# A decoder layer with a product-key expert FFN: loads of the expert stage pinned in program order, own slots for the U tiles, gates read in parts

## The chip, the cores and the metric

The kernel runs on one core of one Trainium2 chip. What counts is the device time of one execution in microseconds (us). Of the kernel before, three runs are known: median 1809.51 us, from 1806.57 to 1817.64 us.

## The reference, cut to what matters

512 tokens of 1024 numbers pass through one layer: a mixer, and behind it an expert FFN in which every token picks, for each of 8 heads, 16 of 16,384 experts. Each expert has a row in `expert_u` and one in `expert_v`.

```python
q = (xc @ w_q).reshape(PEER_CHUNK, PEER_HEADS, 2, PEER_HALF)
s1 = einsum('thd,hnd->thn', q[:, :, 0], sub_keys_1)      # 128 keys per half
s2 = einsum('thd,hnd->thn', q[:, :, 1], sub_keys_2)
...                                                      # top 16 of both, top 16 of their sums
g = jax.nn.softmax(top_s, axis=-1)
u_sel = jnp.take(expert_u, idx, axis=0)
act = jax.nn.gelu(jnp.einsum('thkd,td->thk', u_sel, xc))
v_sel = jnp.take(expert_v, idx, axis=0)
return jnp.einsum('thk,thkd->td', g * act, v_sel)
...
h = h + hybrid_mixer(n, ...)
h = h + peer(rms_norm(h, norm_ffn), ...)
return rms_norm(h, norm_final)
```

All values are float32.

## The kernel before

**Arithmetic.** A float32 matrix product is done as three matmul passes over a high and a low part of each operand. A weight tile of 128x1024 float32 (512 KB) is loaded by SP's DMA queue into a slot `raw` (L80, four slots), ACT copies it to `whi` (L74), and VectorE (DVE) subtracts to get `wlo` (L75; for some tiles GpSimd, POOL, does that). `whi` and `wlo` have three slots each. TensorE (PE) then uses both.

**Expert FFN.** For the first 384 tokens (three groups of 128) the experts are not gathered: all 128 tiles of 128 experts are multiplied with all these tokens, and the result is weighted by a gate that is zero where an expert was not chosen. For tile j, `act_tile(j)` loads the U tile and makes the gelu of its products (24 matmuls, L89, L377), and `out_tile(j)` loads the V tile, multiplies the activations with the gates (DVE, L638), splits the product into `w_hi` (ACT, L74) and `w_lo` (DVE, L75), and adds 18 matmuls onto six PSUM banks `acc` (L645). The last 128 tokens are done by gathers: 128 indirect DMAs by POOL (L402), each bringing one row of U and V per token (1 MB, slot `row`, four of them), and on DVE a dot product with each (`junk`, L409) and a weighted sum (`yg`, L396), in a fixed order.

**Stages.** Mixer (0 to 500 us); queries and top 16 (500 to 690); decoding of the indices (690 to 765); the gates stage, which builds the gate matrix in 48 blocks of 8 tokens (L571 to L596: four DVE instructions, L564 and L566, and 16 small matmuls, L583 and L584, a block; every fourth block a DMA stores 2 MB, `stg`, into the DRAM array `gscr`, L592); the expert stage (1006 to 1798), and the closing normalisation `finish` (L612).

**Tiles done ahead.** The U tiles of 74 of the 128 j, the list `LAG`, are computed before the expert stage by `lag_tiles` (L382): 20 in the top-16 stage, 12 while decoding, 42 between the blocks of the gates stage. Of the first 12 (`keep`) the activations stay in SBUF; the others are stored to DRAM (`ascr`, L389) and read again in the expert stage into a slot `back` (L661, four slots), two tiles ahead in the program (`PRE = 2`).

**Order.** In the expert stage the program goes through j: read the `back` of j+2, compute the U tile of j if it was not done ahead, then `out_tile(j-1)`, then some gathered rows. The gates of four tiles are read by one DMA of 768 KB in runs of 512 bytes (`gt`, L634), two slots, at the `out_tile` that uses them first. PE runs in program order. A scheduler orders the other engines and SP's queue, except for instructions pinned by `keep_in_program_order`; each engine, and SP's queue, then works strictly in its order. A DMA whose slot is still in use blocks all behind it in SP's queue. SP's slot waits are mostly for the `wlo` that read a `raw` slot last.

Of the kernel before, what the change touches and what calls it, by code (L numbers as in the profile page):

```python
# [21 lines left out]
P = 128  # L22
D = 1024
# [13 lines left out]
NG = ND // TG  # L37
JG = 4
NL = 74
LAG = [j for j in range(P) if j * NL // P != (j - 1) * NL // P]  # L40
# [6 lines left out]
AR = 20  # L47
AD = 4
UP = 24
PRE = 2  # L50
C_VEC = dict(nm=0, nf=8, ca=16, rw=40, rb=80, brg=90, big=100, lam=110)
# [4 lines left out]
def layer(ctx: ExitStack, tc: tile.TileContext, a):  # L56
# [20 lines left out]

    def weights(src, k, eng=None):
        raw = ring.tile([P, k * P], F32, tag="raw", name="raw", bufs=4)
        SP.dma_start(raw, src)  # L80
        hi, lo = split(raw, [P, k * P], ("whi", "wlo"), ring, 3, eng)
        return hi.rearrange("p (k m) -> p k m", k=k), lo.rearrange("p (k m) -> p k m", k=k)
# [285 lines left out]

    def act_tile(j):
        u = weights(a["ut"][j], KD, G if j in LAG[:AR] else V)  # L370
        pa = bank("01", (P, S))
        mm3(pa[:, :ND], u, n2d)
        if j in LAG[:JK]:
            g = gp.tile([P, ND], F32, tag="keep", name="keep", bufs=JK)
        else:
            g = gp.tile([P, ND], F32, tag="gel", name="gel", bufs=3)
        A.activation(g, pa[:, :ND], AF.Gelu_apprx_tanh)  # L377
        return g
# [20 lines left out]
    def gathered(i, pin=False):  # L399

        r = gp.tile([P, 2 * D], F32, tag="row", name="row", bufs=4)
        ins = G.indirect_dma_start(  # L402
            out=r, out_offset=None, in_=a["uv"], in_offset=bass.IndirectOffsetOnAxis(ap=uidx[:, i : i + 1], axis=0)
        )
        if pin:
            tc.keep_in_program_order(ins)
        junk = gp.tile([P, D], BF16, tag="junk", name="junk", bufs=1)
        tc.keep_in_program_order(
            V.scalar_tensor_tensor(junk, r[:, :D], 1.0, n2tok, op0=ALU.mult, op1=ALU.mult, accum_out=dots[:, i : i + 1])  # L409
        )  # L410
# [140 lines left out]
    with tc.tile_pool(name="gates", bufs=1) as rp:  # L551
# [17 lines left out]
        blocks = [(t, t0) for t in range(NT) for t0 in range(0, P, TE)]  # L569
        ahead = rows_of(*blocks[0])  # L570
        for n, (t, t0) in enumerate(blocks):  # L571
            e2, eh, el = ahead
# [18 lines left out]
            if s0 + TE == TG:  # L591
                SP.dma_start(gscr[t * (P // TG) + c], stg)  # L592
            left = NL - AR - AD * NT
            lag_tiles((n + 1) * left // len(blocks) - n * left // len(blocks))
            for i in range(n * UP // len(blocks), (n + 1) * UP // len(blocks)):
                gathered(i)  # L596


# [4 lines left out]
    def residual(k):  # L603
        hk = ep.tile([P, S], F32, tag="hk", name="hk", bufs=2)
        SP.dma_start(hk, hscr[:, k, :])
        c = (k % 4) * P
# [4 lines left out]

    def finish(t, parts):  # L612
        sq = ep.tile([P, S], F32, tag="fsq", name="fsq", bufs=2)
        ss = ep.tile([P, 2], F32, tag="fss", name="fss", bufs=2)
        A.activation(sq, parts[0], AF.Square, accum_out=ss[:, 0:1])
        A.activation(sq, parts[1], AF.Square, accum_out=ss[:, 1:2])
        s1 = ep.tile([P, 1], F32, tag="fs1", name="fs1", bufs=2)
# [3 lines left out]
        o = ep.tile([P, D], F32, tag="fo", name="fo", bufs=2)  # L621
        for f in range(2):
            fs = slice(f * S, (f + 1) * S)
            V.scalar_tensor_tensor(o[:, fs], parts[f], s1, gfin[:, fs], op0=ALU.mult, op1=ALU.mult)
            SP.dma_start(a["out"][t * P : (t + 1) * P, fs], o[:, fs])
# [39 lines left out]
    work.append(lambda: finish(3, [yg[:, :S], yg[:, S:]]))  # L665
    share = [1.0 if j in LAG else RN for j in range(P)]
# [4 lines left out]
    for j in range(P + 1):  # L671
        if j < P:
            read_back(j + PRE)
            g = kept[j] if j in LAG else act_tile(j)
            part += share[j]
# [5 lines left out]
        while done < min(len(work), math.ceil(part * len(work) / total)):  # L681
            work[done]()
            done += 1
    for t in range(NT):
        finish(t, acc[t])

# [48 lines left out]
```

## Time and profile before

| | |
|---|---|
| median of 3 runs | 1809.51 us (1806.57 to 1817.64) |
| the profiled execution, its own time | 1809.08 us |
| its span in the trace | 1807.4 us |
| busy share PE, DVE, ACT, POOL | 96%, 71%, 42%, 18% |
| expert stage | 1006 to 1798 us |

The profile is one execution seen by the hardware profiler. The page gives the busy time of each engine; a table by windows gives it by stage, with the granted TensorE clock (PEclk, 1.00 is full) and the busy share of the 16 DMA engines. The list of waits groups an engine's idle time by what ended it: "DVE back L638 <- DMA back<-ascr" is DVE standing at the gate multiply until the read of `back` had landed. The chain of waits goes back from the last instruction to what released it, and shows which of these waits set the end; in it a DMA piece runs from its issue to its landing. 1.7 us of the execution lie outside the span.

### The profile page before, as it was taken

How to read it: one execution, taken by the hardware profiler on the slowest of the kernel's cores; microseconds unless marked ns; L12 is line 12 of the kernel's file. 1: busy time of each engine (PE TensorE's matmuls, PEld its weight loads, DVE VectorE, ACT ScalarE, POOL GpSimd, SP SyncE). 2: the span in 40 equal slices, each digit the busy share in tenths (PEclk: the TensorE clock that was granted, in tenths of full speed). 3: DMA queues.
4: the chain of work that ended last, by engine and by line, in shares of the span. 5: the costliest groups of instructions: out<-in, count | busy, mean ns of one | idle time of the engine just before them, and what ended most of it. 6: DMA issues, size and time to landing. Idle time of an engine off the chain costs nothing.

```text
span 1807.4 us, 24072 instructions
## 1 busy us (share of the span) xinstructions
PE 1736.7 (96%) x8861; PEld 1515.1 (84%) x8861; DVE 1286.5 (71%) x2345; ACT 763.8 (42%) x1290; POOL 320.2 (18%) x253
## 2 busy tenths in 40 slices
PE   8999999999989998999999899999899999999998
PEld 6888888888879887999999688788787878888786
DVE  7979442225578668899997777787676866787673
ACT  5774332222343335555554343344343433444353
POOL 0000000000145552023222111122121111122100
PEclk9999999999999998999999999999999999999999
DMA  4323223333433335579999988898898988898872
GB/s 164 114 82 111 96 79 95 107 105 94 134 114 96 103 120 199 171 307 357 376 367 369 347 309 312 297 332 313 283 322 295 323 289 309 310 344 313 308 239 72
DMA packets 147846, 410.06 MB, mean 227 GB/s; under 512 B 11536, under 2 KB 78864, under 8 KB 129680
## 3 DMA queue, kind: packets, MB, share of 16 engines
q1 hardware_dynamic: 129296, 274.30, 45.5%
q0 software_dynamic: 18432, 134.23, 19.2%
q8 instruction: 69, 1.13, 0.2%
q14 instruction: 49, 0.40, 0.1%
HBM read 366.93 MB, written 41.55 MB: 226 GB/s over the span
## 4 chain that ended last, share of the span: by engine, by line
PE 78%; DMA 9%; DVE 8%; issue 2%; ACT 2%; SPq 0%; DVEq 0%; ACTq 0%
PE ps L89 55%; PE acc L645 19%; DMA back<-ascr 5%; DMA gt<-gscr 3%; DVE wlo L75 3%; PE ps L583 1%; PE ps L584 1%; PE ps L517 1%; ACT whi L74 1%; PE ps L236 1%; DVE gel L638 1%; DMA gscr<-stg 1%; ACT w_hi L74 1%; DVE junk L409 1%; DVE nk L141 0%
## 5 line engine op out<-in xcount | busy, mean ns | idle before, releaser
L74 ACT ACTIVATE whi<-raw 128x1024 fp32r<-128x1024 f32 (+1 forms) x364 | 380.6, 1046 | 693.9 <-PE ps L89 479.5
L75 DVE TENSOR_TENSOR wlo<-raw,whi 128x1024 fp32r<-128x1024 f32 (+1 forms) x328 | 393.0, 1201 | 219.1 <-ACT whi L74 218.5
L89 PE MATMUL ps<-q_hi,whi 128*128 128x384 f32 (+1 forms) x1232 | 436.4, 354 | 11.6 <-ACT whi L74 8.9
L89 PE MATMUL ps<-q_hi,wlo 128*128 128x384 f32 (+1 forms) x1232 | 430.0, 349 | 6.1 <-DVE wlo L75 6.1
L89 PE MATMUL ps<-q_lo,whi 128*128 128x384 f32 (+1 forms) x1232 | 429.8, 349 | 0.3 <-DVE q_lo L143 0.3
L402 POOL DMA_INDIRECT row<-uv,uidx x128 | 210.2, 1642 | 766.9 <-DVE yg L396 757.5
L645 PE MATMUL acc<-whi,w_hi 128*128 128x512 f32 x768 | 245.9, 401 | 37.9 <-ACT w_hi L74 37.3
L89 PEld LDWEIGHTS ps<-q_hi,whi 128*128 128x128 f32 x1232 | 234.6, 190 | 24.3 <-ACT whi L74 10.2
L89 PEld LDWEIGHTS ps<-q_hi,wlo 128*128 128x128 f32 x1232 | 234.2, 190 | 17.1 <-DVE wlo L75 8.1
L89 PEld LDWEIGHTS ps<-q_lo,whi 128*128 128x128 f32 x1232 | 234.8, 191 | 11.1 <-DVE q_lo L143 0.7
L645 PE MATMUL acc<-wlo,w_hi 128*128 128x512 f32 x768 | 241.6, 396 | 0.0
L645 PE MATMUL acc<-whi,w_lo 128*128 128x512 f32 x768 | 240.9, 395 | 0.0
L645 PEld LDWEIGHTS acc<-whi,w_hi 128*128 128x128 f32 x768 | 144.9, 192 | 70.8 <-ACT w_hi L74 45.6
L645 PEld LDWEIGHTS acc<-wlo,w_hi 128*128 128x128 f32 x768 | 147.6, 192 | 32.2
L645 PEld LDWEIGHTS acc<-whi,w_lo 128*128 128x128 f32 x768 | 146.5, 191 | 31.5
L89 PE MATMUL ps<-n_hi,whi 128*128 128x512 f32 x432 | 168.4, 390 | 0.0
L89 PE MATMUL ps<-n_hi,wlo 128*128 128x512 f32 x432 | 168.2, 390 | 0.0
L89 PE MATMUL ps<-n_lo,whi 128*128 128x512 f32 x432 | 168.1, 389 | 0.0
L396 DVE SCALAR_TENSOR_TENSOR yg<-row,dots,yg 128x1024 f32<-128x1024 f32 x128 | 163.9, 1280 | 0.0
L409 DVE SCALAR_TENSOR_TENSOR junk<-row,n2tok 128x1024 bf16<-128x1024 f32 x128 | 156.0, 1219 | 0.0
L75 POOL TENSOR_TENSOR wlo<-raw,whi 128x1024 fp32r<-128x1024 f32 x36 | 87.2, 2424 | 349.8 <-ACT whi L74 349.8
L89 PEld LDWEIGHTS ps<-n_hi,wlo 128*128 128x128 f32 x432 | 81.1, 188 | 17.5 <-DVE wlo L75 0.4
(208 smaller groups left out, 1891.7 us busy)
## 6 DMA issues: line engine op xcount, KB each, us to landing
raw<-ut SPq DMA_DIRECT2D x128, 512.0 KB
raw<-uv SPq DMA_DIRECT2D x128, 512.0 KB
raw<-w_in SPq DMA_DIRECT2D x60, 512.0 KB
gscr<-stg SPq DMA_DIRECT2D x12, 2048.0 KB
gt<-gscr SPq DMA_DIRECT2D x32, 768.0 KB
ascr<-gel SPq DMA_DIRECT2D x62, 192.0 KB
back<-ascr SPq DMA_DIRECT2D x62, 192.0 KB
raw<-w_q SPq DMA_DIRECT2D x16, 512.0 KB
```

The lines of the kernel that those rows point to most:

```text
L74: A.activation(hi, raw, AF.Copy)
L75: (lo_eng or V).tensor_sub(lo, raw, hi.bitcast(F32))
L89: T.matmul(ps, w[x][:, i, :], r[y][i], start=first and n == 0, stop=last and n == 3 * k - 1)
L236: T.matmul(pg, x[:, s * P : (s + 1) * P], y, start=n == 0, stop=n == 2)
L396: V.scalar_tensor_tensor(yg, r[:, D:], dots[:, i : i + 1], yg, op0=ALU.mult, op1=ALU.add)
L402: ins = G.indirect_dma_start(out=r, out_offset=None, in_=a["uv"], in_offset=bass.IndirectOffsetOnAxis(ap=uidx[:, i : i + 1], axis=0))
L409: V.scalar_tensor_tensor(junk, r[:, :D], 1.0, n2tok, op0=ALU.mult, op1=ALU.mult, accum_out=dots[:, i : i + 1])
L517: T.matmul(psc[:, s * P : (s + 1) * P], qs[s][:, t * P : (t + 1) * P], keys[:, 2 * hd + s, :], start=True, stop=True)
L583: T.matmul(o, e2[:, ti // 2, :, ti % 2], eh[:, ti // 2, :, ti % 2], start=True, stop=False)
L584: T.matmul(o, e2[:, ti // 2, :, ti % 2], el[:, ti // 2, :, ti % 2], start=False, stop=True)
L638: V.tensor_mul(g.rearrange("p (c t) -> p c t", t=TG), g.rearrange("p (c t) -> p c t", t=TG), gt)
L645: T.matmul(acc[t][f], w[x][:, t * P : (t + 1) * P], vf[y][:, f * S : (f + 1) * S], start=nout == 0 and (x, y) == (0, 0), stop=nout == P - ...
```

## The change

The program's lines move: SP's loads are now at L82, the split at L75 (`whi`) and L76 (`wlo`, `w_lo`), the gate multiply at L667, `junk` at L418, `yg` at L405, the stores of `ascr` at L398 and of `gscr` at L603.

- Loads issued by SP in the expert stage (V and U tiles, `back`, `gt`, the residual) are pinned in program order.
- U tiles of the expert stage get three slots of their own, `rawu`; V tiles keep the four slots `raw` alone.
- Gates are read for eight tiles at a time (`JG = 8`), in four parts of 384 KB in runs of 1 KB, one part at each of the last four tiles before the group; the first group is read in six parts.
- `back` gets five slots, and is read one tile ahead in the program instead of two (`PRE = 1`).
- 76 instead of 74 U tiles are done ahead; four of them now stand behind the last block of the gates stage (`AT = 4`), so 40 instead of 42 stand between the blocks.
- POOL instead of DVE makes `wlo` of four more tiles (the first four of the decode stage).
- The store of the gates goes in four parts of 512 KB, two per block. `row` has three slots instead of four.
- The output of the gathered tokens is stored at the end of the program, and `finish` uses existing tiles for its squares and its output.

```diff
-JG = 4
-NL = 74
+JG = 8
+NL = 76
...
+AT = 4
 UP = 24
-PRE = 2
+PRE = 1
...
+    def load(out, src):
+        i = SP.dma_start(out, src)
+        if pinned[0]:
+            tc.keep_in_program_order(i)
+
+    def weights(src, k, eng=None, raw=None):
+        if raw is None:
+            raw = ring.tile([P, k * P], F32, tag="raw", name="raw", bufs=4)
+        load(raw, src)
...
-        u = weights(a["ut"][j], KD, G if j in LAG[:AR] else V)
+        u = weights(a["ut"][j], KD, G if j in LAG[:AR + AD] else V, raw)
...
-        r = gp.tile([P, 2 * D], F32, tag="row", name="row", bufs=4)
+        r = gp.tile([P, 2 * D], F32, tag="row", name="row", bufs=3)
...
-                SP.dma_start(gscr[t * (P // TG) + c], stg)
-            left = NL - AR - AD * NT
+                stores += [
+                    lambda i=i, c=t * (P // TG) + c, stg=stg: SP.dma_start(gscr[c, :, i : i + P // 4, :], stg[:, i : i + P // 4, :])
+                    for i in range(0, P, P // 4)
+                ]
+            for _ in range(2):
+                if stores:
+                    stores.pop(0)()
+            left = NL - AR - AD * NT - AT
...
+        while stores:
+            stores.pop(0)()
+        lag_tiles(AT)
...
+    def read_gates(n, c0, c1):
+
+        if n * JG >= P:
+            return
+        if c0 == 0:
+            gst[n] = ep.tile([P, NG, JG, TG], F32, tag="gt", name="gt", bufs=2)
+        load(gst[n][:, c0:c1], gscr[c0:c1, :, n * JG : (n + 1) * JG, :].rearrange("c p j t -> p c j t"))
+
     def out_tile(j, g):
         nonlocal nout
-        if j % JG == 0:
-            gst["g"] = ep.tile([P, NG, JG, TG], F32, tag="gt", name="gt", bufs=2)
-            SP.dma_start(gst["g"], gscr[:, :, j : j + JG, :].rearrange("c p j t -> p c j t"))
-        gt = gst["g"][:, :, j % JG, :]
+        k = j % JG
+        if j == 0:
+            for c in range(0, NG, 2):
+                read_gates(0, c, c + 2)
+        if k >= 4:
+            read_gates(j // JG + 1, 3 * k - 12, 3 * k - 9)
+        gt = gst[j // JG][:, :, k, :]
...
+    pinned[0] = True
...
-            kept[j] = ep.tile([P, ND], F32, tag="back", name="back", bufs=PRE + 2)
-            SP.dma_start(kept[j], ascr[j])
+            kept[j] = ep.tile([P, ND], F32, tag="back", name="back", bufs=5)
+            load(kept[j], ascr[j])
...
-            g = kept[j] if j in LAG else act_tile(j)
+            g = kept[j] if j in LAG else act_tile(j, ep.tile([P, D], F32, tag="rawu", name="rawu", bufs=3))
```

**Reads of `back` in SP's queue.** A piece of SP's order about a sixth into the expert stage, before. The number at a name tells its tiles apart; a load waits until the slot that it takes has been read (the slot of `raw` comes round after four loads).

```order
L80 DMA raw_10533<-uv 128x1024
L661 DMA back_10607<-ascr_79 128x384
L80 DMA raw_10571<-uv 128x1024
L80 DMA raw_10609<-uv 128x1024
L80 DMA raw_10645<-ut 128x1024
L634 DMA gt_10778<-gscr_78 128x12x128
L80 DMA raw_10678<-uv 128x1024
L661 DMA back_10714<-ascr_79 128x384
L80 DMA raw_10716<-uv 128x1024
L80 DMA raw_10745<-ut 128x1024
```

And of the change, at about the same tile:

```order
L82 DMA back_10648<-ascr_79 128x384
L82 DMA rawu_10650<-ut 128x1024
L82 DMA raw_10683<-uv 128x1024
L82 DMA back_10719<-ascr_79 128x384
L82 DMA raw_10721<-uv 128x1024
L82 DMA raw_10757<-uv 128x1024
L82 DMA back_10786<-ascr_79 128x384
L82 DMA rawu_10788<-ut 128x1024
L82 DMA raw_10821<-uv 128x1024
```

Before, `back_10714` stands behind `raw_10678`, which takes the slot of `raw_10533`, four loads earlier. Of the change, `back_10786` stands behind the V tile `raw_10757`, which takes the slot of `raw_10575`, four V loads earlier. U tiles no longer take part in this count. In the whole stage a `back` stands right behind a V load in 62 of the change's 64 reads.

**The gate multiply on DVE.** The same places in DVE's order, before:

```order
L75 TENSOR_TENSOR wlo_10536<-raw_10533,whi_10535 128x1024
L75 TENSOR_TENSOR w_lo_10541<-back_10353,w_hi_10540 128x384
L409 SCALAR_TENSOR_TENSOR junk_10564,dots_3822<-row_10562,n2tok_3823 128x1024
L396 SCALAR_TENSOR_TENSOR yg_3824<-row_10491,dots_3822,yg_3824 128x1024
L638 TENSOR_TENSOR back_10607<-back_10607,gt_10778 128x384
L75 TENSOR_TENSOR wlo_10574<-raw_10571,whi_10573 128x1024
L638 TENSOR_TENSOR back_10714<-back_10714,gt_10778 128x384
L75 TENSOR_TENSOR wlo_10612<-raw_10609,whi_10611 128x1024
L638 TENSOR_TENSOR gel_10531<-gel_10531,gt_10569 128x384
L75 TENSOR_TENSOR w_lo_10579<-gel_10531,w_hi_10578 128x384
```

And of the change:

```order
L76 TENSOR_TENSOR wlo_10578<-raw_10575,whi_10577 128x1024
L405 SCALAR_TENSOR_TENSOR yg_3824<-row_10532,dots_3822,yg_3824 128x1024
L76 TENSOR_TENSOR wlo_10615<-raw_10612,whi_10614 128x1024
L667 TENSOR_TENSOR back_10786<-back_10786,gt_10466 128x384
L76 TENSOR_TENSOR wlo_10653<-rawu_10650,whi_10652 128x1024
L667 TENSOR_TENSOR gel_10572<-gel_10572,gt_10057 128x384
L76 TENSOR_TENSOR w_lo_10620<-gel_10572,w_hi_10619 128x384
```

Before, `wlo_10536` frees the slot that lets SP come to `back_10714`, and the multiply of `back_10714` stands behind the next `wlo`, `wlo_10574`. Of the change, `wlo_10578` frees the slot that lets SP come to `back_10786`, and its multiply stands behind the next `wlo` too, `wlo_10615`; a further `wlo` and the multiply of a `gel` stand behind it. Counted over the stage, with such a distance of exactly one `wlo` between the release and the use stand 17 of 62 reads of `back` before and 44 of 64 of the change; of the reads of gates 14 of 32 before and 2 of 59 of the change; of the `raw` loads none in either (three between them before, four or more of the change).

**From the gates stage to the expert stage, in SP's queue.** Before, from the store before the last one on:

```order
L389 DMA ascr_79<-gel_9152 128x384
L80 DMA raw_9443<-uv 128x1024
L389 DMA ascr_79<-gel_9219 128x384
L80 DMA raw_9479<-uv 128x1024
L592 DMA gscr_78<-stg_9040 128x4096
L389 DMA ascr_79<-gel_9274 128x384
L80 DMA raw_9515<-ut 128x1024
L601 DMA gfin_9288<-nfin 128x1024
L634 DMA gt_9336<-gscr_78 128x12x128
L634 DMA gt_9548<-gscr_78 128x12x128
```

And of the change, from the last block's stores on:

```order
L603 DMA gscr_78<-stg_9003 128x1024
L398 DMA ascr_79<-gel_9283 128x384
L620 DMA gfin_9392<-nfin 128x1024
L82 DMA rawu_9407<-ut 128x1024
L398 DMA ascr_79<-gel_9317 128x384
L82 DMA gt_9440<-gscr_78 128x2x256 x4
L398 DMA ascr_79<-gel_9351 128x384
L82 DMA gt_9440<-gscr_78 128x2x256 x2
L82 DMA raw_9447<-uv 128x1024
L82 DMA raw_9483<-uv 128x1024
```

Before, the V tiles `raw_9338`, `raw_9374` and `raw_9443` are issued ahead of the last store of gates. Of the change, the first V tile stands behind the `ascr` store of the third of the four tiles that now follow the last block.

## Rows read from the trace of the kernel before

**Rows 1.** Windows table, by stage; columns as its second line says.

```profile
core 0: us, PE busy (x) PEld busy (x) DVE busy (x) ACT busy (x) POOL busy (x), PEclk, DMA share, GB/s
690.00:765.00 75.00, 67.53 (x382) 65.18 (x381) 69.20 (x166) 39.71 (x60) 8.68 (x11) 0.93 0.59 189
765.00:980.00 215.00, 215.00 (x1710) 208.58 (x1706) 213.67 (x297) 112.44 (x222) 58.70 (x24) 1.00 0.91 351
980.00:1006.00 26.00, 16.16 (x91) 15.12 (x90) 6.80 (x9) 7.63 (x12) 1.17 (x1) 0.87 0.97 335
...
1006.00:1799.00 793.00, 762.73 (x3600) 661.47 (x3599) 578.20 (x747) 318.70 (x578) 145.38 (x100) 0.98 0.85 297
```

**Rows 2.** Waits of PE, 1000 to 1808 us; columns: total, times, longest us.

```profile
PE acc L645 <- ACT w_hi L74: 37.3, 13, 8.2
```

**Rows 3.** Waits of DVE in the same stretch.

```profile
DVE back L638 <- DMA back<-ascr: 42.3, 13, 5.9
DVE back L638 <- DMA gt<-gscr: 37.1, 17, 5.3
DVE keep L638 <- DMA gt<-gscr: 7.9, 3, 4.8
...
DVE back L638 <- DMA raw<-uv: 4.1, 1, 4.1
```

**Rows 4.** Timeline of SP; columns: start us, us, engine, line, op, count.

```profile
1139.02 0.33 SPq L80 DMA_DIRECT2D raw<-uv  x1
1139.49 0.34 SPq L661 DMA_DIRECT2D back<-ascr  x1
```

**Rows 5.** Chain of waits, 1120 to 1800 us: three of its twelve back rows.

```profile
1139.49 10.39 DMA back<-ascr
...
1288.33 11.41 DMA back<-ascr
...
1651.87 3.95 DMA back<-ascr
```

**Rows 6.** Timeline of DVE at that place; idle time ahead in brackets.

```profile
1137.77 1.22 DVE L75 TENSOR_TENSOR wlo<-raw,whi 128x1024 fp32r<-128x1024 f32 x1
...
1149.97 0.56 DVE L638 TENSOR_TENSOR back<-back,gt 128x384 f32<-128x384 f32 x1 [5.45 <-DMA back<-ascr]
...
1151.58 0.55 DVE L638 TENSOR_TENSOR gel<-gel,gt 128x384 f32<-128x384 f32 x1
```

**Rows 7.** Timeline of PE at that place.

```profile
1152.74 1.09 PE L645 MATMUL acc<-whi,w_hi 128*128 128x512 f32 x2 [3.88 <-ACT w_hi L74]
```

**Rows 8.** Chain of waits in a gapless stretch of the expert stage.

```profile
1057.72 4.09 PE acc L645 x18
...
1110.42 4.16 PE ps L89 x24
```

**Rows 9.** Groups by line: the split on DVE (gates stage), on POOL (all).

```profile
L75 DVE TENSOR_TENSOR wlo<-raw,whi 128x1024 fp32r<-128x1024 f32 x41 | 50.0, 1220 | 3.6 <-ACT whi L74 3.3
...
L75 POOL TENSOR_TENSOR wlo<-raw,whi 128x1024 fp32r<-128x1024 f32 x36 | 87.2, 2424 | 349.8 <-ACT whi L74 349.8
```

**Rows 10.** Gathered rows: issue to landing, gates stage, then expert stage.

```profile
DMA to landing us min/median/max: 10.0/12.0/15.3
...
DMA to landing us min/median/max: 5.9/8.8/11.2
```

**Rows 11.** Chain of waits, end of the gates stage; columns: start us, us, what.

```profile
982.83 13.18 DMA gscr<-stg
...
996.54 2.20 DMA gt<-gscr
...
1005.67 4.36 PE acc L645 x10
```

**Rows 12.** The profile page: all DMA packets, and the queue of SP.

```profile
DMA packets 147846, 410.06 MB, mean 227 GB/s; under 512 B 11536, under 2 KB 78864, under 8 KB 129680
...
q1 hardware_dynamic: 129296, 274.30, 45.5%
```

More of the change, by code (lines that the diff above doesn't have):

```diff
@@ L76, in split @@
         return hi, lo
-    def weights(src, k, eng=None):
-        raw = ring.tile([P, k * P], F32, tag="raw", name="raw", bufs=4)
-        SP.dma_start(raw, src)
+    pinned = [False]
+    def load(out, src):
[6 more added lines that the diff above has]
+        load(raw, src)
         hi, lo = split(raw, [P, k * P], ("whi", "wlo"), ring, 3, eng)
@@ L367, in layer, with act_tile @@
     kept = {}
-    def act_tile(j):
-        u = weights(a["ut"][j], KD, G if j in LAG[:AR] else V)
+    def act_tile(j, raw=None):
+        u = weights(a["ut"][j], KD, G if j in LAG[:AR + AD] else V, raw)
         pa = bank("01", (P, S))
@@ L570, in layer @@
         ahead = rows_of(*blocks[0])
+        stores = []
         for n, (t, t0) in enumerate(blocks):
@@ L604, in residual @@
         hk = ep.tile([P, S], F32, tag="hk", name="hk", bufs=2)
-        SP.dma_start(hk, hscr[:, k, :])
+        load(hk, hscr[:, k, :])
         c = (k % 4) * P
@@ L610, in residual, with finish @@
             )
[L612 to L617, printed above, removed]
+    def finish(t, parts, o, junk):
+        ss = ep.tile([P, 2], F32, tag="fss", name="fss", bufs=3)
+        for f in range(2):
+            A.activation(junk[:, f * S : (f + 1) * S], parts[f], AF.Square, accum_out=ss[:, f : f + 1])
+        s1 = ep.tile([P, 1], F32, tag="fs1", name="fs1", bufs=3)
         V.tensor_add(s1, ss[:, 0:1], ss[:, 1:2])
@@ L624, in finish @@
             V.scalar_tensor_tensor(o[:, fs], parts[f], s1, gfin[:, fs], op0=ALU.mult, op1=ALU.mult)
-            SP.dma_start(a["out"][t * P : (t + 1) * P, fs], o[:, fs])
+            if t < NT:
+                SP.dma_start(a["out"][t * P : (t + 1) * P, fs], o[:, fs])
     nout = 0
     gst = {}
+    def read_gates(n, c0, c1):
[4 more added lines that the diff above has]
+        load(gst[n][:, c0:c1], gscr[c0:c1, :, n * JG : (n + 1) * JG, :].rearrange("c p j t -> p c j t"))
     def out_tile(j, g):
         nonlocal nout
-        if j % JG == 0:
-            gst["g"] = ep.tile([P, NG, JG, TG], F32, tag="gt", name="gt", bufs=2)
-            SP.dma_start(gst["g"], gscr[:, :, j : j + JG, :].rearrange("c p j t -> p c j t"))
-        gt = gst["g"][:, :, j % JG, :]
+        k = j % JG
[5 more added lines that the diff above has]
+        gt = gst[j // JG][:, :, k, :]
         v = weights(a["uv"][j * P : (j + 1) * P, D:], KD, V)
@@ L659, in read_back @@
             j = spilled.pop(0)
-            kept[j] = ep.tile([P, ND], F32, tag="back", name="back", bufs=PRE + 2)
-            SP.dma_start(kept[j], ascr[j])
+            kept[j] = ep.tile([P, ND], F32, tag="back", name="back", bufs=5)
+            load(kept[j], ascr[j])
     work = [lambda i=i: gathered(i) for i in range(UP, HK)]
     work.append(gathered_sum)
-    work.append(lambda: finish(3, [yg[:, :S], yg[:, S:]]))
+    work.append(lambda: finish(3, [yg[:, :S], yg[:, S:]], yg, gp.tile([P, D], BF16, tag="junk", name="junk", bufs=1)))
     share = [1.0 if j in LAG else RN for j in range(P)]
@@ L683, in layer @@
             done += 1
+    fo = ep.tile([P, NG, JG, TG], F32, tag="gt", name="fo", bufs=2).rearrange("p c j t -> p (c j t)")
+    load(a["out"][NT * P :, :], yg)
     for t in range(NT):
-        finish(t, acc[t])
+        o = fo[:, t * D : (t + 1) * D]
+        finish(t, acc[t], o, o)
 def tiles(w, k, m):
```

1 line of the change is left out of this document (removed).

## The prediction

> **What bounds the kernel now.** I read the table by windows first. In the expert stage, 1006 to 1799 us, PE is busy 762.73 of 793.00 us at a granted clock of 0.98, so 30.3 us are idle, 0.6 us of them behind its last matmul [rows 1]. In the gates stage PE has no gap (215.00 of 215.00) and DVE is close behind (213.67); in the decode stage PE is idle 75.00 - 67.53 = 7.5 us while DVE is busy 69.20; in the 26 us between gates and experts PE is idle 9.8 us at 0.87 of the clock [rows 1]. So PE's own work is the bound, and a change that neither adds nor removes work can win or lose only about 48 us of gaps.
>
> Then I asked what PE waits for in the expert stage. It is the `w_hi` copy on ACT, 13 times [rows 2]; but ACT only hands on a wait of DVE: the gate multiply stood for `back` 42.3 us in 13 waits, for gates 37.1 + 7.9 us in 20 waits, and for a V tile once, 4.1 us [rows 3]. Sum 91.4 us. So a microsecond of DVE standing there costs PE 30.3 / 91.4 = 0.33 us on average.
>
> One place shows why it is not always lost. At 1137.77 DVE starts the `wlo` that frees a raw slot; at 1139.02 SP issues the V load that needed this slot and at 1139.49 the `back` queued behind it [rows 4, 6]. That `back` lands 10.39 us later [rows 5], and DVE, in order, stands at its multiply until 1149.97 (5.45 us) with the multiply of a `gel` behind it at 1151.58 [rows 6]. PE needed that `gel`, not the `back`: it starts again at 1152.74, having stood 3.88 us [rows 7]. A landing after 10.39 - 3.88 = 6.5 us would have cost PE nothing. The pieces of order shown are this place and its like in the change.
>
> **The tight reads.** In both orders this pattern is "exactly one `wlo` between release and use". `wlo` follows PE's pace of one tile, 4.09 or 4.16 us [rows 8]. Before, 17 + 14 = 31 reads of `back` and gates are so tight, against 33 waits seen on DVE for them [rows 3]: the count explains the waits. The change has 2 tight reads of gates for 14, but 44 of `back` for 17, because each `back` now stands right behind a V load, and that always waits for a slot. The deeper raw slots themselves buy little: the `raw` loads made DVE wait once [rows 3].
>
> **The terms.**
>
> Expert stage. The 17 tight `back` gave 42.3 us of DVE waits, 2.5 us each; the 14 tight gate reads 45.0 us, 3.2 us each [rows 3]. With the same landings the change has 44 x 2.5 + 2 x 3.2 = 116 us, times 0.33 = 38 us of idle PE for 30: +8. How the landings change no row shows, so I bound it. The gates before move in 32 x 768 KB / 512 B = 49,152 packets, as I count them; the change needs half, 24,576 fewer. If a packet costs the same whatever its size, it is 0.455 x 16 x 1807.4 / 129296 = 0.10 us of one DMA engine [rows 12], so 24,576 x 0.10 / 16 = 156 us of each engine; if bytes alone count, nothing. The queue's mean packet is 2.1 KB, so a 512-byte one is well below the mean; I take a third, some 50 us of 793, or 6 points of a DMA share of 0.85 [rows 1]. Gathered rows land after 12.0 us at a share of 0.91 and after 8.8 us at 0.85 [rows 10], half a microsecond a point, but those two stages differ in much else. I take 0.5 us off each landing in all: 44 x 2.0 + 2 x 3 = 94 us, times 0.33 = 31 us, **+1**. Bounds: -25 (all land within 6.5 us; some 5 us are left) and +33 (the slow rival below).
>
> The Trainium skill, "DMA: Bandwidth & Descriptors", section "Specifications", speaks against a gain here: it puts the smallest transfer at line rate at 512 B, and the old runs were just that. By it the term would be the +8 of unchanged landings and the whole 7 us later than my sum; by the mean price per packet above it would be below +1. The page's whole count of packets under 2 KB, 78,864 [rows 12], fits either.
>
> Gates stage. Two U tiles leave, 2 x 4.16 = 8.3 us of PE work [rows 8]. But DVE loses only 2 of its `wlo`, 1.22 us each [rows 9], and had 213.67 us of work for PE's 215.00 [rows 1]: it becomes the bound at about 211 us, so the stage shortens by 4 us while PE's work falls by 8: **+4**. Row slots go from four to three: a gather is issued when the `yg` three rows earlier, not four, has run. With 24 rows in 215 us, 9 us apart, and `yg` one row behind `junk`, that leaves two spacings, 18 us, instead of 27, and less where the order has them closer, for a landing of 10.0 to 15.3 us [rows 10]. Some rows come late for a DVE that now has no slack: from 0 to 24 rows x 1 us; I take **+4**. In the expert stage landing is 8.8 us and DVE has slack; 0.
>
> The seam. The last store of gates is issued at 982.83, lands 13.18 us later, the gates are read at 996.54, and PE starts on the experts at 1005.67 [rows 11]: 23 us, of which PE was idle 9.8. The change puts four tiles, 16.6 us, behind the last block, so the three tiles there before become six, 25 us, and the store behind the last block is 512 KB parts instead of 2 MB. That covers the 23 us. But the first V tile is issued only after the third of these tiles, and has about as long to land as two or three tiles take; I leave 1 us idle, and 1 us is won back where the clock had been at 0.87: **-10**, from -11 to -5.
>
> Decode stage. Four `wlo` move from DVE (1.22 us) to POOL (2.4 us) [rows 9], which is busy 8.68 of 75 us [rows 1]. DVE, the busier of the two there, falls by 4.9 us; PE can win no more than its 7.5 us idle, and the top of the chain there is decode work: **-3**, from 0 to -5.
>
> At no cost: the two tiles more done ahead are the same PE work elsewhere, and the two more `ascr` stores and reads of 192 KB are 0.8 MB of 410. The order of the final instructions on ACT and DVE is unchanged; the store of the gathered tokens moves past the last V loads in SP's queue and lies beside the last tiles. With that cover gone, it would cost its landing, some 2 us.
>
> Sum: +1 + 4 + 4 - 10 - 3 = -4 on the profiled execution of 1809.1 us, which lies 0.4 us under the median of the runs: **1805 us**.
>
> **Rivals.**
>
> *Slower: a `back` behind a V load lands later.* Twelve `back` reads stand on the chain, from 3.95 to 11.41 us, 7.9 us on average [rows 5]. They are the late ones, but in the change almost every `back` is issued half a microsecond behind a 512 KB load, as that of 10.39 us was. At 7.9 us each of 44 costs PE 7.9 - 6.5 = 1.4 us, 62 us for 30, **+33** for +1: 1837 us. It decides from a mean landing of 7.6 us, where 44 x 1.1 = 48 us, and the sum passes 1%. Against it: only 13 of 17 tight reads waited at all [rows 3]. The Trainium skill, same page, "Queues, rings and completion order", says that a DMA engine takes the descriptors of a ring in their order, so a `back` stands behind its V tile's bytes; the 10.39 us agree, but are one read.
>
> *Faster: landings fall under 6.5 us.* With the gates' packets halved and issued a tile or more earlier, tight reads cease to matter: stage -25 for +1, the rest as above or without the late rows, 1775 to 1779 us. For it: gates alone made half of the DVE waits [rows 3]. Against it: 44 reads for 17.
>
> *Rows.* If the three row slots also hold back DVE in the expert stage, 100 gathers x 1 us x 0.33 is +33 with the multiply waits unchanged, near 1838 us; a landing of 8.8 us with a maximum of 11.2 [rows 10] with DVE busy 578 of 793 us [rows 1] speaks against it.
>
> *Nothing moves:* DVE waits change places, seam and gates stage cancel: 1809 us, inside the forecast.
>
> **How the numbers follow.** Forecast with its neighbours, 1792 to 1827 us (1% of 1809 is 18 us, about what a measurement can tell from no change): 0.42. Faster rival, with mixtures of it that pass 1%: 0.33. Slow rival 0.17, rows 0.08: slower 0.25. Mixtures lie between the extremes, so the range 1776 to 1836 leaves out some 2 in 10. The likeliest case's own range is 1796 to 1816.
>
> **What would show it.** Right: in the changed profile 30 to 50 waits of DVE for `back` and hardly any for gates; PE's idle time in the expert stage near 31 us; between gates and experts under 3 us; the gates stage bound by DVE with 3 to 8 us of gaps in PE. Wrong: DVE waits for `back` far over 100 us (slow rival), or under 50 us (fast one); waits at `junk` for rows in the expert stage; PE waiting at its first V tile.

## The result, and the profile after

The change made the kernel slower: 1900.8 us median (1900.02 to 1905.25, 4 runs) against 1808.0 us of the kernel before (4 runs), a ratio of 1.0515 (95% interval 1.0462 to 1.0568). The profiled execution has a span of 1898.1 us, 90.7 us more than before.

Table by windows of the changed kernel; the columns are busy time and count of PE, PEld, DVE, ACT and POOL, then the granted TensorE clock, the DMA share and GB/s:

```profile
690.00:765.00 75.00, 67.55 (x386) 65.71 (x385) 70.82 (x158) 38.02 (x58) 18.83 (x14) 0.93 0.57 177
765.00:1002.00 237.00, 216.36 (x1661) 207.56 (x1660) 207.91 (x289) 112.07 (x216) 117.35 (x23) 0.94 0.86 313
1002.00:1034.50 32.50, 26.14 (x140) 25.22 (x138) 9.46 (x14) 7.70 (x14) 0.94 (x1) 0.95 0.84 296
1034.50:1889.20 854.70, 782.87 (x3576) 670.15 (x3576) 580.01 (x744) 319.14 (x576) 149.56 (x101) 0.96 0.77 278
```

The last row answers to the expert stage of [rows 1]. It takes 854.7 us for 792.7 before (1005.7 to 1798.4), although one U tile fewer is left in it. PE is idle 71.8 us in it for 29.7 before, and its clock is 0.96 for 0.98, so the same matmuls also last longer. The gates stage, which had no gap before, has 20.6 us of them at a clock of 0.94.

Waits of DVE in the changed kernel, 1000 to 1900 us (engine, line, what it waited for: total, times, longest us), answering to [rows 3]:

```profile
DVE back L667 <- DMA back<-ascr: 110.0, 42, 4.9
...
DVE back L667 <- issue: 17.1, 4, 5.8
DVE junk L418 <- DMA row<-uv,uidx: 16.4, 12, 4.0
DVE back L667 <- DMA raw<-uv: 16.0, 3, 8.9
DVE back L667 <- DMA gt<-gscr: 6.2, 2, 3.4
...
DVE keep L667 <- DMA gt<-gscr: 3.1, 1, 3.1
```

Waits of PE in the same stretch, answering to [rows 2]:

```profile
PE acc L674 <- ACT w_hi L75: 36.4, 21, 5.2
PE acc L674 <- DVE w_lo L76: 34.8, 11, 4.6
```

DVE waits at the multiply for `back` 42 times, for gates hardly any more; PE now also waits for `w_lo`, which only DVE makes. In the gates stage DVE waits for gathered rows, and PE for DVE:

```profile
DVE junk L418 <- DMA row<-uv,uidx: 27.5, 10, 5.9
```

```profile
PE ps L593 <- DVE ehl L575: 17.6, 6, 5.0
```

Where the 90.7 us arose, from landmarks in both traces (first and last copy of the gates out of PSUM; first and last `acc` matmul). PE work that moved between stages, at 4.16 us a U tile, is taken out in the last column but one:

| stretch | before us | after us | difference | without moved tiles | forecast |
|---|---|---|---|---|---|
| up to the first gates | 764.6 | 762.1 | -2.5 | -2.5 | -3 |
| gates stage | 217.3 | 239.6 | +22.3 | +30.6 (two tiles fewer) | +8 |
| seam | 23.8 | 32.8 | +9.0 | -3.5 (three more) | -10 |
| expert stage | 792.7 | 854.7 | +62.0 | +66.2 (one fewer) | +1 |
| closing | 9.0 | 8.9 | -0.1 | -0.1 | 0 |

One place in the expert stage of the changed kernel, in the timelines of SP, DVE and PE (start us, us, engine, line, op; idle time ahead in brackets):

```profile
1591.44 0.33 SPq L82 DMA_DIRECT2D raw<-uv  x1
1591.82 1.10 SPq L82 DMA_DIRECT2D back<-ascr  x1
...
1595.39 0.33 SPq L82 DMA_DIRECT2D raw<-uv  x1
1595.77 0.54 SPq L82 DMA_DIRECT2D back<-ascr  x1
```

```profile
1594.14 1.22 DVE L76 TENSOR_TENSOR wlo<-raw,whi 128x1024 fp32r<-128x1024 f32 x1
...
1598.50 0.56 DVE L667 TENSOR_TENSOR back<-back,gt 128x384 f32<-128x384 f32 x1 [2.67 <-DMA back<-ascr]
1598.97 1.22 DVE L76 TENSOR_TENSOR wlo<-raw,whi 128x1024 fp32r<-128x1024 f32 x1
...
1604.73 0.56 DVE L667 TENSOR_TENSOR back<-back,gt 128x384 f32<-128x384 f32 x1 [4.07 <-DMA back<-ascr]
1605.21 0.55 DVE L76 TENSOR_TENSOR w_lo<-gel,w_hi 128x384 fp32r<-128x384 f32 x1
```

```profile
1601.27 0.73 PE L674 MATMUL acc<-whi,w_hi 128*128 128x512 f32 x2 [0.71 <-ACT w_hi L75]
...
1605.82 1.10 PE L674 MATMUL acc<-whi,w_lo 128*128 128x512 f32 x2 [3.35 <-DVE w_lo L76]
```

It is the pattern of [rows 4 to 7], twice in a row. `back` is issued at 1591.82 and at 1595.77, each 0.4 us behind a V load that had to wait for its slot; DVE reaches their multiplies too soon and stands 2.67 and 4.07 us. PE stands 0.71 us after the first. Behind the second multiply stands the `w_lo` that PE needs, and PE stands 3.35 us.

### The profile page after: what moved, and what is told of

Its sections match the earlier page's. It is cut to its first block, busy times and chain, and to the rows that moved or that the text cites. A ratio compares the mean times of both kernels' runs of the same rounds, so it can differ in the third digit from the quotient of the medians.

```text
span 1898.1 us, 24090 instructions
## 1 busy us (share of the span) xinstructions
PE 1769.8 (93%) x8861; PEld 1534.8 (81%) x8861; DVE 1290.0 (68%) x2341; ACT 765.6 (40%) x1290; POOL 392.8 (21%) x257
## 4 chain that ended last, share of the span: by engine, by line
PE 50%; DMA 14%; issue 14%; DVE 11%; POOL 7%; ACT 2%; SPq 1%; DVEq 0%; POOLq 0%; ACTq 0%
PE ps L98 37%; PE acc L674 11%; DMA back<-ascr 7%; POOL row L411 7%; DMA gt<-gscr 4%; DVE wlo L76 4%; DVE junk L418 2%; DVE yg L405 1%; DMA rawu<-ut 1%; DMA raw<-uv 1%; SPq L82 1%; PE ps L526 1%; ACT whi L75 1%; PE ps L245 1%; DVE w_lo L76 1%
## 5 line engine op out<-in xcount | busy, mean ns | idle before, releaser
L75 ACT ACTIVATE whi<-raw 128x1024 fp32r<-128x1024 f32 (+1 forms) x312 | 325.6, 1044 | 596.7 <-PE ps L98 376.2
L76 DVE TENSOR_TENSOR wlo<-raw,whi 128x1024 fp32r<-128x1024 f32 (+1 forms) x272 | 325.1, 1198 | 172.8 <-ACT whi L75 170.6
L411 POOL DMA_INDIRECT row<-uv,uidx x128 | 270.9, 2116 | 794.6 <-DVE yg L405 781.0
L674 PE MATMUL acc<-whi,w_hi 128*128 128x512 f32 x768 | 252.4, 411 | 39.6 <-ACT w_hi L75 36.4
L674 PE MATMUL acc<-whi,w_lo 128*128 128x512 f32 x768 | 250.4, 408 | 34.8 <-DVE w_lo L76 34.8
L674 PE MATMUL acc<-wlo,w_hi 128*128 128x512 f32 x768 | 248.2, 405 | 0.5 <-DVE wlo L76 0.5
L674 PEld LDWEIGHTS acc<-whi,w_hi 128*128 128x128 f32 x768 | 148.9, 198 | 76.2 <-ACT w_hi L75 45.8
L674 PEld LDWEIGHTS acc<-whi,w_lo 128*128 128x128 f32 x768 | 151.4, 199 | 72.0 <-DVE w_lo L76 39.5
L418 DVE SCALAR_TENSOR_TENSOR junk<-row,n2tok 128x1024 bf16<-128x1024 f32 x128 | 156.2, 1220 | 44.0 <-DMA row<-uv,uidx 43.9
L76 POOL TENSOR_TENSOR wlo<-raw,whi 128x1024 fp32r<-128x1024 f32 x40 | 98.5, 2467 | 355.8 <-ACT whi L75 355.8
L405 DVE SCALAR_TENSOR_TENSOR yg<-row,dots,yg 128x1024 f32<-128x1024 f32 x128 | 163.9, 1280 | 0.0
L667 DVE TENSOR_TENSOR back<-back,gt 128x384 f32<-128x384 f32 x64 | 35.4, 557 | 149.3 <-DMA back<-ascr 110.0
```

The source lines that it names most:

```text
L75: A.activation(hi, raw, AF.Copy)
L76: (lo_eng or V).tensor_sub(lo, raw, hi.bitcast(F32))
L405: V.scalar_tensor_tensor(yg, r[:, D:], dots[:, i : i + 1], yg, op0=ALU.mult, op1=ALU.add)
L411: ins = G.indirect_dma_start(out=r, out_offset=None, in_=a["uv"], in_offset=bass.IndirectOffsetOnAxis(ap=uidx[:, i : i + 1], axis=0))
L667: V.tensor_mul(g.rearrange("p (c t) -> p c t", t=TG), g.rearrange("p (c t) -> p c t", t=TG), gt)
L674: T.matmul(acc[t][f], w[x][:, t * P : (t + 1) * P], vf[y][:, f * S : (f + 1) * S], start=nout == 0 and (x, y) == (0, 0), stop=nout == P - ...
```

## The experiments

Times are given against the kernel before, run beside each. "Stage" is the expert stage, from the first to the end of the last `acc` matmul in the trace.

**Row slots alone.** The kernel before with three row slots.

```diff
-        r = gp.tile([P, 2 * D], F32, tag="row", name="row", bufs=4)
+        r = gp.tile([P, 2 * D], F32, tag="row", name="row", bufs=3)
```

> The kernel before with three row slots instead of four, nothing else. Theory (row slots make the gates stage long): a gather starts a row later, its instruction on POOL falls on a busy DVE, DVE waits at junk for rows, and the time from 765 us to the last small matmul grows from 211 us by 20 to 30 us as it did in the changed kernel (where it grew by 26 us with two U tiles fewer); total 1830 to 1840 us. Rival (the stage grew because of the split stores and the new order of the blocks): 211 us within 3, total 1805 to 1813 us.

Measured: 1823.8 us, ratio 1.0067 (1.0044 to 1.0089), some 12 us slower. The last copy of the gates out of PSUM starts at 988.7 us for 981.9 before, 6.8 us later and not 20 to 30. DVE's waits for rows in the gates stage of this kernel:

```profile
DVE junk L409 <- DMA row<-uv,uidx: 8.9, 7, 2.6
```

The rest lies in the expert stage (801.6 us for 792.7), where DVE now waits for rows too:

```profile
DVE junk L409 <- DMA row<-uv,uidx: 11.0, 6, 3.3
```

Both theories missed: three slots alone explain a part of the gates stage's loss. By the durations of the instructions between them in DVE's order, the `yg` that lets a gather go and the `junk` that needs the row are never nearer than 13 us here; in the changed kernel, every third pair is 10.7 us apart. The rhythm of three comes with the 40 tiles among the 48 blocks: it is there in every kernel with 40, also with four slots, where the nearest pair is 22 us apart. The gathers' own instructions take longer in those kernels too (last section), and no run separates the two.

**The multiply in its program place.** The changed kernel with one instruction pinned: the gate multiply on DVE. SP's queue, slots and loads are as in the change.

```diff
-        V.tensor_mul(g..., g..., gt)
+        tc.keep_in_program_order(V.tensor_mul(g..., g..., gt))
```

> The changed kernel, with the gate multiply on DVE pinned in program order, so that it no longer stands ahead of work that is needed sooner; SP's queue is unchanged. Seven or more wlo then stand between the release and the use of all 64 reads of back, where 44 had one. Theory (tight reads of back cost the expert stage its 62 us): DVE's waits for back at the multiply fall from 110 us in 42 to under 10 us, the expert stage from 855 to 765 to 785 us, total 1815 to 1835 us. Rival (the loss is contention of the DMA queues, or late rows, whatever DVE's order): expert stage above 835 us, total above 1880 us.

Measured: 1794.4 us, ratio 0.9907 (0.9879 to 0.9936), 106 us faster than the change. DVE no longer waits for `back` or gates at the multiply at all; it still waits for rows. That wait from 1000 us on, and windows of this kernel, expert stage and gates stage:

```profile
DVE junk L418 <- DMA row<-uv,uidx: 19.5, 17, 3.0
```

```profile
1036.90:1783.40 746.50, 744.95 (x3576) 650.83 (x3576) 582.62 (x748) 322.23 (x576) 157.27 (x101) 1.00 0.87 317
765.00:1006.50 241.50, 219.03 (x1671) 210.10 (x1670) 209.58 (x292) 113.10 (x219) 118.50 (x23) 0.95 0.85 308
```

The stage is 746.5 us with 1.6 us of idle PE and a clock of 1.00: shorter than expected, because the clock came back too. The gates stage is as slow as in the change. So the 108 us between 854.7 and 746.5 hung on where the multiply stands in DVE's order: SP's loads stand in the very same order in both traces. The waits for rows, 17.6 of the 19.5 us inside the stage, cost PE next to nothing here.

**The same for the kernel before.**

```diff
-        V.tensor_mul(g..., g..., gt)
+        tc.keep_in_program_order(V.tensor_mul(g..., g..., gt))
```

> The kernel before with the gate multiply pinned in program order, nothing else. Theory (tight reads cost the kernel before 30 us of PE idle in the expert stage): no DVE waits for back or gates, PE idle there under 8 us, total 1775 to 1788 us. Rival (the multiply then comes late itself and PE waits for w_hi): 1805 us or more.

Measured: 1761.7 us, ratio 0.9734 (0.9711 to 0.9758). The stage:

```profile
1003.70:1750.40 746.70, 746.67 (x3600) 655.03 (x3600) 580.61 (x746) 324.56 (x577) 158.16 (x100) 1.00 0.88 315
```

No idle PE is left: 746.7 us for 792.7. The gain of 46 us is more than the 30 us of idle time; the other 16 us are PE work that now runs at the full clock (746.67 for 763.03 us busy). I had expected a gain at least 13 us smaller. In this kernel the loads are not pinned, and the scheduler changed SP's order along with DVE's; the changed kernel above, where SP's order stayed, is the cleaner test.

**Pinning alone.** The kernel before with the loads of the expert stage pinned.

```diff
-        SP.dma_start(raw, src)
+        i = SP.dma_start(raw, src)
+        if pinned[0]:
+            tc.keep_in_program_order(i)
...                                   (back, gt and hk likewise)
```

> The kernel before with only the loads of the expert stage pinned in program order, slots unchanged (PRE 2, four raw slots shared). By the order no read of back is then one wlo from its release (17 before), and 4 of 32 reads of gates (14 before). Theory (the count of reads one wlo apart tells the DVE waits): DVE waits for back and gates fall from 87 us to 20 to 40 us, total 1785 to 1800 us. Rival (pinning itself makes the queue block more, and is what made the change slow): total above 1825 us.

Measured: 1835.5 us, ratio 1.0144 (1.01 to 1.0189): slower, not faster. The theory's number missed by 35 us, and the rival's came out. Waits of DVE and PE in this kernel:

```profile
DVE back L642 <- DMA gt<-gscr: 60.9, 16, 8.8
...
DVE keep L642 <- DMA gt<-gscr: 15.8, 4, 5.6
```

```profile
PE acc L649 <- DVE w_lo L75: 31.9, 7, 5.6
PE acc L649 <- ACT w_hi L74: 17.4, 6, 6.7
```

As the order had said, no wait for `back` is left. But the gates, of which most are now two `wlo` from their release, wait longer: the gate reads on the chain of waits take 11.3 us on average from issue to landing (11 of them from 1120 us on) for 8.7 us before (6). Of the 20 waits for gates in the trace, 15 belong to reads two `wlo` from their release. So the distance has to be held against the landing of that load, not against one number. Why they land later with the loads pinned stays open.

**Four row slots in the change.** To make room, its U tiles share the four raw slots.

```diff
-..., name="row", bufs=3)
+..., name="row", bufs=4)
-            g = kept[j] if j in LAG else act_tile(j, ep.tile(..., tag="rawu", name="rawu", bufs=3))
+            g = kept[j] if j in LAG else act_tile(j)
```

> The changed kernel with four row slots again; to make room in SBUF its U tiles share the four raw slots as in the kernel before. By the order 42 of 64 reads of back are one wlo from their release (44 in the changed kernel), and a gather is issued at least 22 us of DVE work before its junk in the gates stage (from 10.7 us in the changed kernel, 20 us in the kernel before, 13 us in the kernel before with three row slots). Theory: the gates stage (765 us to the last small matmul) loses its 34 us and ends near 972 us instead of 1002, with no DVE waits for rows there; the expert stage stays at 845 to 875 us, since raw slots of its own do nothing for it; total 1860 to 1880 us. Rival (raw slots of their own for U tiles matter): expert stage above 880 us or under 830 us.

Measured: 1911.1 us, ratio 1.0548 (1.0509 to 1.0586). The gates stage is cured (last copy at 974.4 us, no wait for rows), as the theory said. The stage is not 845 to 875 but 893 us, the rival's side. The edit changes two things, and the run doesn't tell which of them made the stage longer. DVE's waits:

```profile
DVE back L667 <- DMA back<-ascr: 139.0, 42, 6.8
...
DVE back L667 <- DMA gt<-gscr: 21.5, 5, 5.4
```

42 waits for 42 reads that stood one `wlo` from their release, as counted, but of 3.3 us each for 2.6 in the change.

**Both cures in the change.**

```diff
-..., name="row", bufs=3)
+..., name="row", bufs=4)
-            g = kept[j] if j in LAG else act_tile(j, ep.tile(..., tag="rawu", name="rawu", bufs=3))
+            g = kept[j] if j in LAG else act_tile(j)
-        V.tensor_mul(g..., g..., gt)
+        tc.keep_in_program_order(V.tensor_mul(g..., g..., gt))
```

> The same (four row slots, U tiles in the shared raw slots) with the gate multiply pinned. If the two causes, multiplies that stand too early and rows that come late, are all that made the change slow, both gains add: gates stage ends near 972 us, expert stage 745 to 755 us, total 1755 to 1765 us, no slower than the kernel before with the multiply pinned (1761.7 us). Rival (another part of the change costs time too, the split gate reads or the pinned loads): 1775 us or more.

Measured: 1761.3 us, ratio 0.973 (0.9692 to 0.9767).

```profile
1006.50:1750.10 743.60, 743.55 (x3576) 651.75 (x3576) 581.45 (x748) 323.86 (x575) 156.88 (x100) 1.00 0.88 317
765.00:976.50 211.50, 209.63 (x1680) 202.59 (x1680) 210.21 (x293) 114.60 (x221) 134.19 (x23) 1.00 0.95 352
```

Both gains add, as expected. Once the multiply and the rows are right, the pinned loads and the split reads cost nothing in the expert stage: PE has no gap there. They are not free elsewhere: the next kernel, without them, is 7.6 us faster, most of it between the gates and the experts, where this one leaves PE some 6 us idle.

**The seam, in the fast version.** The kernel before with the multiply pinned, and of the change only the four tiles behind the gates (76 ahead) and POOL's `wlo` for four tiles.

```diff
+AT = 4
-NL = 74
+NL = 76
...
-            left = NL - AR - AD * NT
+            left = NL - AR - AD * NT - AT
...
+        lag_tiles(AT)
...                                   (POOL's `wlo`; the multiply pinned as above)
```

> The kernel before with the multiply pinned, and of the change only the four tiles behind the last block of gates (76 done ahead) and POOL's wlo for four tiles more. Theory (the seam's idle 10.3 us are hidden by the tiles): idle of PE between the last small matmul and the first V tile falls from 10.3 to 1 to 6 us, gates stage without gaps, total 1750 to 1758 us. Rival (with 40 instead of 42 tiles DVE becomes the bound of the gates stage and gives it all back): 1760 to 1765 us.

Measured: 1753.6 us, ratio 0.9679 (0.9645 to 0.9713), the fastest of all, 3.2% under the kernel before and 8 us under the pinned multiply alone.

```profile
765.00:975.50 210.50, 208.62 (x1674) 201.58 (x1673) 209.06 (x293) 113.40 (x219) 134.23 (x23) 1.00 0.94 352
975.50:1000.60 25.10, 23.62 (x137) 23.30 (x136) 7.86 (x9) 6.87 (x12) 0.94 (x1) 1.00 1.00 379
```

The seam has 25.10 - 23.62 = 1.5 us of idle PE left, and the gates stage, with 40 tiles and four row slots, 1.9 us: 40 tiles with four slots did it no harm.

**Reading `back` two tiles ahead again**, in the change (`PRE = 2`).

```diff
-PRE = 1
+PRE = 2
```

> The changed kernel with back read two tiles ahead again (PRE 2, five slots). By the order 28 reads of back instead of 44 are one wlo from their release. Theory (cost by the count of tight reads): DVE waits for back fall from 110 us in proportion to 60 to 80 us, the expert stage loses 110 us over the pinned multiply in the changed kernel and would lose 60 to 80 here: 805 to 830 us, total 1850 to 1875 us. Rival (the count does not set it): expert stage within 10 us of 855 us.

Measured: 1893.5 us, ratio 1.0443 (1.0401 to 1.0486), 7 us faster than the change where 25 to 50 were expected; the intervals of the two ratios overlap. The stage is within 10 us of the change's, as the rival had it. DVE's waits:

```profile
DVE back L667 <- DMA back<-ascr: 102.3, 29, 6.7
...
DVE junk L418 <- DMA row<-uv,uidx: 28.5, 17, 4.3
```

The count holds again (28 tight reads, 29 waits), the proportion does not: 3.5 us each for 2.6, and 12 us more for rows. All its waits for loads inside the stage are 158.9 us, for 166.6 in the change.

**Four tiles ahead, in the kernel before** (`PRE = 4`, six slots).

```diff
-PRE = 2
+PRE = 4
```

> The kernel before with back read four tiles ahead (PRE 4, six slots), DVE's order left to the scheduler. By the order no read of back is fewer than four wlo from its release (17 were one wlo from it), while 16 of 32 reads of gates are one wlo from it (14 before). Theory (a read one wlo from its release is what makes DVE wait): DVE waits for back 0, for gates some 40 to 50 us as before, PE idle in the expert stage 12 to 20 us instead of 30, total 1783 to 1797 us. Rival (waits only move from one load to another, as in the change with PRE 2): DVE waits 75 us or more, total above 1802 us.

Measured: 1772.6 us, ratio 0.9809 (0.9773 to 0.9845), better than expected. No wait for `back` is left, those for gates remain:

```profile
DVE back L638 <- DMA gt<-gscr: 53.5, 19, 5.4
...
DVE keep L638 <- DMA gt<-gscr: 3.3, 2, 2.8
```

These 56.8 us of DVE waits leave 8.0 us of idle PE, 0.14 us for each, where the 86.5 us inside the stage before left 29.7.

**The change without the pinning.**

```diff
-    pinned[0] = True
+    pinned[0] = False
```

> The changed kernel without the pinning of its loads; slots, PRE 1 and gates in parts as in the change. By the order 41 of 64 reads of back are one wlo from their release (44 with the pinning). Theory (the pinning is not what costs, the distance is): 38 to 44 DVE waits for back, expert stage 840 to 880 us, total 1885 to 1925 us. Rival (the pinned queue is what blocks): expert stage under 820 us, total under 1870 us.

Measured: 1872.5 us, ratio 1.0369 (1.0323 to 1.0415), 28 us faster than the change; stage 831.9 us.

```profile
DVE back L667 <- DMA back<-ascr: 83.4, 32, 4.9
...
DVE back L667 <- DMA gt<-gscr: 39.7, 6, 9.3
DVE junk L418 <- DMA row<-uv,uidx: 14.5, 8, 4.2
```

Between theory and rival: the tight reads of `back` are nearly all there, 41 by the order, and 32 waits come of them; the pinning adds some 23 us to the stage, and the rest of the 66 is there without it. In the kernel before, pinning alone added 29 us to the stage; where the multiply is pinned too, nothing. Why the pinned order has more waits (42 for 32) at nearly as many tight reads stays open.

The expert stages side by side. DVE's waits are those at the gate multiply and at `junk`, from the first `acc` matmul on, for a load or with no releaser named. "Busy over full clock" is what PE's busy time exceeds that of the stages without gaps by, 746.7 us with 52 U tiles (the kernels made from the one before) or 743.6 with 51:

| kernel | stage us | DVE waits | PE idle | busy over full clock |
|---|---|---|---|---|
| before, multiply pinned | 746.7 | 0 | 0.0 | 0 |
| change, multiply pinned | 746.5 | 17.6 (rows) | 1.6 | 1.4 |
| before, PRE 4 | 760.0 | 56.8 | 8.0 | 5.4 |
| before | 792.7 | 86.5 | 29.7 | 16.3 |
| before, three row slots | 801.6 | 97.6 | 35.3 | 19.6 |
| before, loads pinned | 821.4 | 83.1 | 49.4 | 25.3 |
| change, not pinned | 831.9 | 148.9 | 63.4 | 24.9 |
| change, PRE 2 | 852.3 | 158.9 | 78.3 | 30.4 |
| change | 854.7 | 166.6 | 71.8 | 39.3 |
| change, four row slots | 893.0 | 185.1 | 95.5 | 53.9 |

## Why the prediction was wrong

The kernel became slower, and in the place that the slow rival named, which had a chance of 0.17. But the rival's mechanism, a `back` that lands later, did not show on the chain of waits, and 1901 us lies far over the 1837 I gave it and outside the range: 92 us over the kernel before, where the rival had 28. The step that failed is the term of the expert stage, +1 forecast and +66 measured. I took 94 us of DVE waits at 0.33 us of idle PE each; there were 167 us at 0.43, and the clock fell with them. The second failure is the term for late rows in the gates stage. How the gap between 28 and 92 divides among the causes below is worked out only in part.

**The count of tight reads was right.** I counted 44 reads of `back` and saw 42 waits of 110.0 us; 44 x 2.5 us of unchanged landings is the same 110. Read by read in the trace, 41 of the 44 tight reads waited, and one of the other 20. The waits for gates went nearly away, 9.3 us for 45.0. With the multiply moved and the order of the reads untouched the loss is gone (1794 us), so multiplies that stand too early are its cause and not, say, contention of the queues. For gates the count was a weaker guide than I wrote: before, only 13 of the 19 waits inside the stage belong to tight reads, and in the kernel before with its loads pinned 4 tight reads went with 20 waits.

**The cut for shorter landings bought nothing.** On the chain of waits the `back` reads did land earlier, after 7.3 us on average (19 of them) for 7.9. But each wait is still 2.6 us long, and my break-even, a landing of 6.5 us that costs PE nothing, came from one wait that stood alone. In the change waits follow closely: at the place shown, 2.67 us and then 4.07 us, their multiplies 6.2 us apart. The first landed 6.7 us after its issue and PE stood only 0.71 us; it had used up the lead that might have forgiven the second. The slow rival's threshold was miscalculated besides: at a mean landing of 7.6 us its sum comes to 13 us over the kernel before, 0.7% and not 1%.

**The idle time of PE was mis-sized in two places.** Forecast 94 us of DVE waits x 0.33 = 31 us of idle PE; measured 166.6 us and 71.8 us. First, the waits for `back` came to 110 us and not 88, and some 50 us of waits were not in my sum: rows with three slots (16.4 us; I had set them at 0 here), V loads (16.0) and waits without a named releaser at the multiply of `back` (17.1). Second, the price of a wait is not constant: the table has 0.14 us of idle PE for each at 57 us of waits, 0.34 at 87, 0.43 at 167, 0.52 at 185. With three slots for `whi` and `wlo`, DVE can be up to three weight tiles ahead of PE; on this reading, single waits use that lead up and waits in close succession go to PE. That is argued and not shown. The kernel with the loads pinned, 0.59 at 83 us, and the change with its multiply pinned, 1.6 us of idle PE at 17.6 us of waits for rows, stand off the line, so what stands behind the waiting instruction may count as well. Why the single waits are longer with PRE 2 (3.5 us) and with four row slots (3.3 us) stays open.

**The clock was left out.** I took the lower clock of the expert stage as given. It came with the gaps: over a stage, each us of idle PE goes with about half a us more of busy time (16.3 / 29.7 before, 39.3 / 71.8 after, 53.9 / 95.5 with four row slots; from 0.4 to 0.7 among the kernels with 8 us of gaps or more; 0 with no gap). That is 23 of the 66 us, and it makes the pinned multiply gain 46 us where the idle time was 30. A place of the changed kernel, PE behind a wait:

```profile
1169.30 1.22 PE L674 MATMUL acc<-whi,w_hi 128*128 128x512 f32 x2 [5.18 <-ACT w_hi L75]
1170.32 1.05 PE L674 MATMUL acc<-wlo,w_hi 128*128 128x512 f32 x2
1171.17 1.05 PE L674 MATMUL acc<-whi,w_lo 128*128 128x512 f32 x2
1172.03 0.84 PE L674 MATMUL acc<-whi,w_hi 128*128 128x512 f32 x2
1172.71 0.63 PE L674 MATMUL acc<-wlo,w_hi 128*128 128x512 f32 x2
1173.17 0.62 PE L674 MATMUL acc<-whi,w_lo 128*128 128x512 f32 x2
```

```profile
1169.00:1171.00 2.00, 1.70 (x4) 1.42 (x5) 1.98 (x4) 1.61 (x3) 0.00 (x0) 0.52 1.01 338
```

After 5.18 us of waiting, pairs of matmuls start 0.85 to 1.02 us apart, then 0.46; the granted clock of the first 2 us is 0.52, near the lower of the two levels (1.2 GHz), and from 1173 us on it is 1.00 again (2.4 GHz). The Trainium skill, "TensorE: Matmul & The Clock Gate", Part 1, says that the throttled state is the default and activity releases it. The rows agree: 0.52 behind an idle PE, 1.00 again once PE had been busy. So a gap of PE cost about half as much again on average.

**The gates stage.** Sign and mechanism were right: DVE becomes the bound, and rows come late. The size was not: +30.6 for +8. DVE as the bound is the small part: where four row slots keep the rows in time, the stage with 40 tiles takes 211 us, some 2 us over what PE's work would give, for the 4 of the forecast. The rest, near 29 us for 4, came with the rows: DVE waited 27.5 us for them, and again the clock (0.94) took part. Three row slots alone cost about 7 us, 40 tiles with four slots 2; together DVE's order puts every third pair 10.7 us apart, under the 12 us median landing of [rows 10]. I had estimated 18 us from the mean spacing instead of reading it in the order.

**The seam** gained 3.5 us, not 10: six tiles cover the chain from store to gates of [rows 11], but PE still stands 32.50 - 26.14 = 6.4 us, mostly at a U tile that waits for a gelu (2.9 us) and ahead of the first V tile (3.2 us). In the fastest version, whose loads are not pinned, 1.5 us remain. **The decode stage** shows 2.5 us for 3, but that can't be told from chance: the first copy of the gates starts at 761.6 to 764.6 us in the five kernels that leave this stage as it was, and at 761.1 to 765.2 us in the seven that have POOL's four `wlo`. The closing cost nothing.

**Landings.** On the chain of waits of the change a `back`, issued some 0.4 us behind its V load, landed 7.3 us after its issue on average. The Trainium skill, "DMA: Bandwidth & Descriptors", "Queues, rings and completion order", says that a DMA engine takes the descriptors of a ring in their order. That fits, but no run here tests it. Whether 1 KB runs are faster than 512-byte ones no run here tells apart either: with the multiply pinned both kinds are hidden.

## What to carry to other kernels

When a scheduler orders an engine, look up where it puts the instruction that consumes a load, and what stands behind it: an early consumer of a late load blocks everything after it, and reading one tile earlier may not help, since the scheduler can move the consumer forward too (28 of 44 reads stayed tight in the change; in the kernel before, four tiles ahead instead of two left none). Pinning the consumer to its program place cost nothing here and took 46 us off the expert stage of one kernel and 108 off that of the other. And look at the clock behind the gaps of PE: over a stage, a gap cost about one and a half times its length here.

## What the hardware showed that was not expected

The gather instruction on POOL takes 1.7 us in the median in the expert stage, but in the gates stage anything from 1.1 to 8.8 us. Its group by line there (765 to 975 us), before, after, and in the fastest version:

```profile
L402 POOL DMA_INDIRECT row<-uv,uidx x22 | 56.5, 2568 | 158.3 <-DVE yg L396 158.3
```

```profile
L411 POOL DMA_INDIRECT row<-uv,uidx x20 | 101.7, 5084 | 111.4 <-DVE yg L405 111.4
```

```profile
L403 POOL DMA_INDIRECT row<-uv,uidx x23 | 134.2, 5836 | 84.6 <-DVE yg L397 84.6
```

The mean goes from 2.6 to 5.1 and 5.8 us, though each gather brings the same amount. It is near 2.5 us in all five kernels with 42 tiles among the blocks and 4.8 to 6.2 us in all seven with 40, whatever the row slots. In the fastest version it does no harm: DVE never waits for a row there. The Trainium skill, "GPSIMD Engine Reference", section "Specifications", says that POOL's SBUF interfaces are shared with VectorE and contend with DVE instructions of two SBUF inputs. No run here shows whether that is the cause. How busy DVE is does not decide it: DVE is busy 99% of this stretch both before and in the fastest version. Spans on POOL are rough besides.
